# Modulation vectors in a two-layer streaming-encoder trunk: where the sums of the last gates are computed, and how the attention paces them

## The chip, the cores and the metric

The kernel runs on one core of one Trainium2 chip. A core has five engines that run side by side: TensorE (PE, matrix products into PSUM), VectorE (DVE), ScalarE (ACT), GpSimd (POOL) and SyncE (SP), which here issues every DMA. Each engine runs its own instructions strictly in order and waits on semaphores for the others. The metric is the device time of one execution in microseconds, the median of several runs.

## What is computed

The trunk has two layers over x of 1024 tokens by 1024 channels. Each layer is a token mixer (layer 0: softmax attention with forget gates, 16 heads; layer 1: gated linear attention, GLA, 4 heads) and a SwiGLU channel mixer with 2816 hidden channels. Six modulation vectors per layer come from one conditioning vector c:

```python
c_act = jax.nn.silu(c)
for i in range(DEPTH):
    mod = c_act @ ada_w[i] + ada_b[i]
    sh1, sc1, g1, sh2, sc2, g2 = jnp.split(mod, N_MOD, axis=-1)
    h = modulate(rms_norm(x, norm1_g[i]), sh1, sc1)
    y = forgetting_attention(h, ...) if i == 0 else gated_linear_attention(h, ...)
    x = x + g1[:, None, :] * y
    h = modulate(rms_norm(x, norm2_g[i]), sh2, sc2)
    x = x + g2[:, None, :] * swiglu(h, ffn_w_in[i], ffn_w_out[i])
return rms_norm(x, final_g)
```

The vectors are numbered j = 0 to 5 in the order of the split. Vectors 0 and 1 of a layer are needed before its token mixer, 2 (g1) behind the token mixer, 3 and 4 ahead of the channel mixer's products, and 5 (g2) only at the very end of the channel mixer. Each vector is the product of c_act (1024) with a 1024 x 1024 block of ada_w, 4 MB of float32.

## The kernel before

All large products are made of three float32r products, high x high, high x low and low x high parts (`mm3`, L266 to L270), so each operand is split into a high part (a cast on ACT) and a low part (a subtraction on DVE or POOL): `split` at L173, and `load_w` at L202 for the weights.

The program is one straight list of instructions. Python generators interleave the stages: `weave` mixes two of them by their given costs, and a framework gives every instruction its semaphores and settles each engine's order by a planned timeline, in which earlier instructions of the list go first when they are ready. `in_order` and `issue_after` fix some of it by hand.

In order of time the kernel does the following. A prologue normalizes x, makes vectors 0 and 1 of layer 0 by its own code and starts the projections. The attention goes through 8 pairs of heads; while pair p is computed (`attention(p)`), the projections of pair p + 1 are woven in (`qk_proj` twice, `v_half` between). Each projection has two halves of 512 tokens, 24 matmuls each, and every half is emptied from its PSUM bank by `q_evac` or `k_evac`. Then come the output projection and the channel mixer of layer 0 (`ffn(0, ...)`, products of 12 matmuls in its first phase), the GLA mixer head by head, and the output projection and channel mixer of layer 1 (`ffn(1, ...)`).

The modulation vectors that the prologue doesn't make are computed by `ada_steps` (L397). One vector is a sum over 1024 rows of ada_w, weighted by c_act. A step takes 32 x nt rows of ada_w, whose 1024 columns lie as four groups of 256 on four groups of 32 partitions of a raw tile (four DMAs from SP, L405), and adds nt weighted sums of 128 x 256 on DVE (L424, L426) onto an accumulator; with nt = 4 a vector takes 8 steps, with nt = 2 it takes 16. At the end matmuls with a 128 x 4 matrix (L431) add the partitions into a PSUM tile of the ring `pj`, and DVE adds the bias (L434).

Each `yield` of `ada_steps` hands a cost to `Pace` (L443), which adds the time that a call gives it and runs steps while its balance is not negative. There are two paces:

- `ada0`, in the attention: vectors 2, 3, 4 and 5 of layer 0 with nt = 4 and no loading ahead. A step is a load and its four sums in one go, at a cost of 1.0. Its raw tiles are taken from `wr`, the ring of three tiles through which the weights of the attention also pass (L208). `qk_proj` calls it with 3.3 behind both halves of each of the 12 projections of pairs 2 to 7 (L1079).
- `ada1`, elsewhere: layer 1's vectors with nt = 2. `mid0` queues vectors 0 and 1 in channel mixer 0, behind its plain first tiles, with three raw tiles and two loads ahead, at costs ADA_A = 6.0 ahead of a step's sums and ADA_B = 3.0 behind them. Every product (`prod`) adds 0.64 for each of its three- or four-deep operand blocks, 2.56 in the first phase. GLA queues vectors 2, 3, 4 and 5 with two raw tiles and one load ahead, at costs 2.5 and 1.0. Behind each half projection of GLA 5.1 is added.

Channel mixer 1 computes no modulation vector. The weights of a channel mixer are fetched up to five operands ahead (`feed.depth = 5`); their sums of blocks are POOL's (L815) and their splits ACT's and DVE's (L174, L175).

Of the kernel before, what the change touches and what calls it, by code (L numbers as in the profile page):

```python
# [20 lines left out]
HALF = 512  # L21
# [32 lines left out]
def trunk(ctx, tc, x, c, ada_w, ada_b, norm1_g, norm2_g, ffn_w_in, ffn_w_out,  # L54
# [54 lines left out]
    def psl(t, n=1):  # L109
        return slice(t * P, (t + n) * P)  # L110
# [161 lines left out]
    def proj(ps, w, hs, hf):  # L272

        cs = hsl(hf)
        for k in range(8):
            mm3(ps, w.hi[:, k, :], w.lo[:, k, :], hs[k].hi[:, cs], hs[k].lo[:, cs], k == 0, k == 7)
            yield 0.65
# [106 lines left out]
    def make_a(l, i, ks=slice(0, 8)):  # L384
        j = 1 if i == 0 else 4
        g0 = 96 + i * 16 + l * 8
        nc.vector.scalar_tensor_tensor(amul[:, l, i, ks], modc[:, l, j, ks], 1.0,
                                       vec[:, g0:g0 + 8][:, ks], op0=ALU.add, op1=ALU.mult)

    def last_of(e):  # L390
        return next(i for i in reversed(nc.cur_bb.bb.instructions) if i.engine == ENG[e])

    def ada_steps(l, j, acc, raw_of, nt, ahead):


        steps, got = deque(range(32 // nt)), deque()

        def load():
            if not steps:
                return  # L400
            n = steps.popleft()
            raw = raw_of([P, nt * 256], F32, f"ada{l}{j}{n}").rearrange("p (t c) -> p t c", t=nt)
            src = ada_w[l, 32 * nt * n:32 * nt * (n + 1), j * D:(j + 1) * D]
            for q in range(4):
                nc.sync.dma_start(raw[32 * q:32 * q + 32],  # L405
                                  src[:, 256 * q:256 * q + 256].rearrange("(r t) c -> r t c", t=nt))
            got.append(raw)

        for _ in range(ahead):
            load()  # L410
        for n in range(32 // nt):
            load()
            if ahead:
                yield ADA_A
            raw = got.popleft()
            with ExitStack() as es:
                if ahead:
                    es.enter_context(tc.issue_after(last_of("D")))
                elif n == 0:
                    es.enter_context(tc.issue_after(split_after["D"]))  # L420
                for t in range(nt):
                    o = (0 if nt == 4 else 32) + t * (32 // nt) + n
                    if n == t == 0:
                        nc.vector.tensor_scalar(acc, raw[:, t], c42[:, o:o + 1], None, op0=ALU.mult)  # L424
                    else:
                        nc.vector.scalar_tensor_tensor(acc, raw[:, t], c42[:, o:o + 1], acc,  # L426
                                                       op0=ALU.mult, op1=ALU.add)
            yield ADA_B if ahead else 1.0
        mp = pj([P, 2, 4], F32, f"mp{l}{j}")
        for b in range(2):  # L430
            nc.tensor.matmul(mp[:, b], acc[:, psl(b)], four, start=True, stop=True)  # L431
        o = l * 48 + j * 8
        qb = lambda t: t.rearrange("p (q b) -> p b q", b=2)
        nc.vector.tensor_add(qb(modc[:, l, j]), mp, qb(vec[:, o:o + 8]))  # L434
        for i, jj in ((0, 1), (1, 4)):
            if j == jj:
                make_a(l, i)
        yield 1.0
# [22 lines left out]

    ada0, ada1 = Pace(), Pace()

    def ada1_queue(js, acc, raws_):
        r = Cycle(raws_)
        for j in js:
            ada1.q.append(ada_steps(1, j, acc, r, 2, len(raws_) - 1))

    mk = mrows[2]
    nc.vector.memset(mk, 0.0)  # L470
# [14 lines left out]
    def new_h(nm):  # L485
        return [Pair(big.tile([P, S], FR, tag=H_SL[2 * k], name=f"{nm}h{k}"),
                     big.tile([P, S], FR, tag=H_SL[2 * k + 1], name=f"{nm}l{k}")) for k in range(8)]
# [231 lines left out]
    def qk_tiles(p):  # L719


        at = {nm: qk_free.popleft() for nm in ("QA", "QB", "KA")}
        if p:
            before = qk_at.pop(p - 1)
            at.update(zip(("KB", "KLA", "KLB"), (before[nm] for nm in ("QA", "KA", "KLA"))))
            qk_free.extend(before[nm] for nm in ("QB", "KB", "KLB"))
        else:
            at.update({nm: qk_free.popleft() for nm in ("KB", "KLA", "KLB")})
        qk_at[p] = at
        return {nm: big.tile([P, S], FR, tag=sl, name=f"{nm}{p}") for nm, sl in at.items()}  # L730
# [338 lines left out]
    def qk_proj(p, i):  # L1069

        if i == 0:
            qkt[p] = qk_tiles(p)
        wt = feed.next()
        feed.depth = 3
        for hf in range(2):
            ps = pj([P, HALF], F32, f"qk{i}{p}{hf}")
            yield from proj(ps, wt, hT, hf)
            (k_evac if i else q_evac)(ps, qkt[p], hf)
        if p > 1:  # L1079
            ada0(3.3)  # L1080

    oTs = {}

# [108 lines left out]
            yield from g  # L1192

    acc0 = acc_r([P, 2, HALF], F32, "acc0")[:, 0, 0:256]
    for j in (2, 3, 4, 5):
        ada0.q.append(ada_steps(0, j, acc0, wr, 4, 0))
    run(v_half(0, 0, gates_end))
    q_evac(accs[1][1][1], qkt[0], 1)
# [4 lines left out]
    for p in range(7):  # L1203
        parts = [qk_proj(p + 1, 0), qk_proj(p + 1, 1)]
        if p < 6:
            parts.insert(1, v_half(p // 2 + 1, p % 2))
        weave(attention(p), 23.0, chain(*parts), 31.0 if p < 6 else 20.8, LAGS)
        load_cum(2 * p + 2)
        load_cum(2 * p + 3)
# [3 lines left out]
    def dump(name, tiles):  # L1213
        if name in dbg:
            for k in range(8):
                nc.sync.dma_start(dbg[name][k], tiles[k])
# [56 lines left out]
    oh = new_h("oh")  # L1273
    x_slots = idle + [list(otr.q)[-1]]
    xs = [big.tile([P, S], F32, tag=x_slots[k], name=f"x0_{k}") for k in range(8)]
# [24 lines left out]
    def ffn_slots(sl):  # L1300
        assert len(sl) == 19
        ex_sl[:] = sl[16:]
        return {"to": sl[0:4], "b": sl[4:12], "hid": sl[12:16]}
# [410 lines left out]
    slots = ffn_slots(rest)  # L1714
# [4 lines left out]
            hs1.extend(new_h("h1"))  # L1719
        return norm_half(xs, ss, hs1, 1, hf, Ring(psp, ["b3", "b4"]), tmp)  # L1720

    def mid0():
        v = Views(slots["hid"], 2, [HALF], "ad0").v
        ada1_queue((0, 1), v[0][:, 0:256], v[1:4])

    ADA_A, ADA_B = 6.0, 3.0
    ffn(0, oh, xs, slots, "fo", mid0, norm_mixer)
    h1 = hs1
    dump("xb0", xs)
    x_d = tc.dram_tile([8, P, S], F32, name="x_d")  # L1730
# [15 lines left out]
    athl = Ring(big, take(1))  # L1746
    s_slot, on_slot = take(2)
    ada_v = Views(take(2), 2, [HALF], "ad").v
    ada1_queue((2, 3, 4, 5), ada_v[0][:, 0:256], ada_v[1:3])
    ADA_A, ADA_B = 2.5, 1.0  # L1750
    rm = ada_v[3]
    nc.vector.memset(rm, 1.0)
    nc.vector.memset(rm.rearrange("p (n c) -> p n c", c=P)[:, :, 0:1], 0.0)
# [247 lines left out]
    oh = new_h("gh")  # L2001
# [8 lines left out]
    xs = [big.tile([P, S], F32, tag=x_slots[k], name=f"x1_{k}") for k in range(8)]  # L2010
# [4 lines left out]
    slots = ffn_slots(rest)  # L2015
# [31 lines left out]
            fzs.append(Views(H_SL[8:16], 2, [HALF], "fz"))  # L2047
        return fzs[0]()

    ffn(1, oh, xs, slots, "go", lambda: None, final_norm, final_scale)  # L2050
    dump("xb1", xs)

# [28 lines left out]
```

## Time and profile before

| what | us |
|---|---|
| median of 3 runs (2403.37, 2404.3, 2410.52) | 2404.3 |
| the profiled execution | 2412.89 |
| its span, from the first to the last instruction | 2411.2 |
| ACT o_s L174, casts of weights, 376 instructions | 217.1 |
| DVE o_s L175, their low parts, 376 instructions | 318.4 |
| ada_s loads, 128 of 128 KB | 2.9 to landing |
| ad_s loads, 384 of 64 KB | 2.4 to landing |

A group of the profile names a line, an engine, an operation and the tiles out<-in, without buffer numbers: `ada_s` is a raw tile of the attention's steps, `ad_s` one of the others' (and `acc_s`, `ad_s` the accumulators), `p_b` a PSUM bank of a channel mixer's product, `s_b` one of attention scores, `kd` GLA's decayed keys, `o_s` split weights of a channel mixer. Behind the bar stand the busy time and the mean of one; then the idle time of the engine before them and who ended it. In views of waits the columns are the total, the number and the longest, in us. A PE that is busy by the profile is not PE at its peak, since the ends of matmuls are modelled.

The stages in the span: the prologue until about 118 us, the attention until about 600 with the output projection from about 480 on, channel mixer 0 until about 1270, GLA until about 1640, its output projection until about 1740 and channel mixer 1 until the end.

### The profile page before, as it was taken

How to read it: one execution, taken by the hardware profiler on the slowest of the kernel's cores; microseconds unless marked ns; L12 is line 12 of the kernel's file. 1: busy time of each engine (PE TensorE's matmuls, PEld its weight loads, DVE VectorE, ACT ScalarE, POOL GpSimd, SP SyncE). 2: the span in 40 equal slices, each digit the busy share in tenths (PEclk: the TensorE clock that was granted, in tenths of full speed). 3: DMA queues.
4: the chain of work that ended last, by engine and by line, in shares of the span. 5: the costliest groups of instructions: out<-in, count | busy, mean ns of one | idle time of the engine just before them, and what ended most of it. 6: DMA issues, size and time to landing. Idle time of an engine off the chain costs nothing.

```text
span 2411.2 us, 35815 instructions
## 1 busy us (share of the span) xinstructions
PE 2376.2 (99%) x12344; PEld 2020.9 (84%) x12344; DVE 1768.2 (73%) x3018; ACT 1128.9 (47%) x2164; POOL 1007.6 (42%) x909
## 2 busy tenths in 40 slices
PE   8999999999999999999999999999999999999998
PEld 7888888888888888888888888888888888888878
DVE  6577778876698788875797676665586767666787
ACT  6666556674443333344325555443343343345326
POOL 1333333333446666643354221222345656653262
PEclk8999999999999999999999999999999999999999
DMA  8432424341435544557654243334324434347664
GB/s 260 137 97 88 124 87 123 107 150 68 149 110 182 176 159 163 181 207 260 228 168 151 76 134 93 100 118 163 122 86 163 171 127 153 131 178 258 230 200 149
DMA packets 335774, 363.43 MB, mean 151 GB/s; under 512 B 24348, under 2 KB 277432, under 8 KB 335592
## 3 DMA queue, kind: packets, MB, share of 16 engines
q1 hardware_dynamic: 335592, 361.15, 45.6%
q8 instruction: 97, 1.59, 0.3%
q14 instruction: 85, 0.70, 0.1%
HBM read 268.19 MB, written 92.86 MB: 150 GB/s over the span
## 4 chain that ended last, share of the span: by engine, by line
PE 79%; DVE 9%; DMA 4%; issue 2%; ACT 2%; SPq 2%; POOL 1%; DVEq 0%; POOLq 0%; ACTq 0%
PE p_b L268 15%; PE p_b L269 15%; PE p_b L270 15%; PE o_b L1150 2%; PE t_b L1136 2%; PE qk_b L268 2%; PE qk_b L269 2%; PE qk_b L270 2%; DMA ad_s<-in_ada_w_dram 1%; PE vps_b L268 1%; PE vps_b L270 1%; PE vps_b L269 1%; SPq L405 1%; PE s_b L1104 1%; PE s_b L1105 1%
## 5 line engine op out<-in xcount | busy, mean ns | idle before, releaser
L174 ACT CAST o_s<-xv_s 128x512 fp32r<-128x512 f32 (+1 forms) x376 | 217.1, 587 | 314.3 <-PE p_b L270 256.1
L175 DVE TENSOR_TENSOR o_s<-xv_s,o_s 128x512 fp32r<-128x512 f32 (+1 forms) x376 | 318.4, 850 | 60.8 <-ACT o_s L174 60.1
L269 PE MATMUL p_b<-B,o_s 128*128 128x512 f32 x608 | 238.6, 392 | 0.0
L270 PE MATMUL p_b<-B,o_s 128*128 128x512 f32 x608 | 237.9, 392 | 0.0
L268 PE MATMUL p_b<-B,o_s 128*128 128x512 f32 x608 | 237.3, 393 | 0.0
L1116 POOL TENSOR_SCALAR lp_s<-lp_s,st 128x128 f32<-128x128 f32 (+7 forms) x128 | 99.0, 778 | 293.4 <-DVE st L1115 280.4
L815 POOL TENSOR_TENSOR ex_s<-xv_s,xv_s 128x512 f32<-128x512 f32 (+1 forms) x64 | 86.8, 1357 | 279.4 <-DMA xv_s<-in_ffn_w_in_dram 112.2
L269 PE MATMUL p_b<-T,o_s 128*128 128x512 f32 x480 | 186.7, 389 | 0.0
L268 PE MATMUL p_b<-T,o_s 128*128 128x512 f32 x480 | 186.7, 389 | 0.0
L270 PE MATMUL p_b<-T,o_s 128*128 128x512 f32 x480 | 181.1, 389 | 0.0
L270 PEld LDWEIGHTS p_b<-B,o_s 128*128 128x128 f32 x608 | 115.2, 190 | 24.1
L268 PEld LDWEIGHTS p_b<-B,o_s 128*128 128x128 f32 x608 | 115.3, 190 | 23.9
L269 PEld LDWEIGHTS p_b<-B,o_s 128*128 128x128 f32 x608 | 115.3, 190 | 23.8
L1114 ACT ACTIVATE lp_s<-lp_s,st 128x128 f32<-128x128 f32 (+7 forms) x128 | 99.3, 776 | 67.0 <-DVE st L1110 64.1
L174 ACT CAST pt_s<-t_b 128x512 fp32r<-128x512 f32 (+1 forms) x160 | 79.7, 548 | 74.7 <-PE t_b L1136 74.0
L1491 DVE TENSOR_TENSOR ex_s<-ex_s,p_b 128x512 f32<-128x512 f32 x140 | 93.7, 680 | 26.9 <-PE p_b L270 26.9
L817 POOL TENSOR_TENSOR xv_s<-ex_s,xv_s 128x512 f32<-128x512 f32 (+1 forms) x64 | 85.6, 1338 | 64.7 <-DVE o_s L175 62.3
L227 POOL TENSOR_TENSOR w_l_s<-w__s,w_h_s 128x256 fp32r<-128x256 f32 x90 | 70.6, 813 | 93.7 <-ACT w_h_s L223 60.4
L175 DVE TENSOR_TENSOR pt_s<-t_b,pt_s 128x512 fp32r<-128x512 f32 (+1 forms) x160 | 96.2, 631 | 15.8 <-ACT pt_s L174 15.1
L268 PEld LDWEIGHTS p_b<-T,o_s 128*128 128x128 f32 x480 | 90.1, 188 | 18.7
L270 PEld LDWEIGHTS p_b<-T,o_s 128*128 128x128 f32 x480 | 90.1, 188 | 18.7
L269 PEld LDWEIGHTS p_b<-T,o_s 128*128 128x128 f32 x480 | 90.1, 188 | 18.6
(1956 smaller groups left out, 7395.4 us busy)
## 6 DMA issues: line engine op xcount, KB each, us to landing
xv_s<-in_ffn_w_in_dram SPq DMA_DIRECT2D x176, 256.0 KB, 3.2
hid_B<-x SPq DMA_DIRECT2D x70, 512.0 KB, 2.6
ad_s<-in_ada_w_dram SPq DMA_DIRECT2D x384, 64.0 KB, 2.4
hid_T<-x SPq DMA_DIRECT2D x36, 512.0 KB, 2.8
xv_s<-in_ffn_w_out_dram SPq DMA_DIRECT2D x96, 192.0 KB, 5.0
ada_s<-in_ada_w_dram SPq DMA_DIRECT2D x128, 128.0 KB, 2.9
xv_s<-in_ffn_w_out_dram SPq DMA_DIRECT2D x40, 256.0 KB, 2.9
T2o<-hid_T SPq DMA_DIRECT2D x18, 512.0 KB, 8.3
```

Source lines behind the costliest of these rows:

```text
L174: nc.scalar.copy(hi, src)
L175: nc.vector.tensor_sub(lo, src, hi.bitcast(F32))
L227: (nc.gpsimd if i < 3 else nc.vector).tensor_sub(lo[:, cs], rw[:, cs], hi[:, cs].bitcast(F32))
L268: nc.tensor.matmul(ps, ah, bh, start=start, stop=False)
L269: nc.tensor.matmul(ps, ah, bl, start=False, stop=False)
L270: nc.tensor.matmul(ps, al, bh, start=False, stop=stop)
L815: nc.gpsimd.tensor_add(s1, a21, a22)
L817: nc.gpsimd.tensor_sub(a11, s1, a11)
L1114: nc.scalar.activation(lp, lp, AF.Exp, bias=mcur, scale=-1.0, accum_out=st[:, qi, 2:3])
L1116: nc.gpsimd.tensor_scalar(lp, lp, st[:, qi, 3:4], 1.0, op0=ALU.mult, op1=ALU.mult)
L1136: nc.tensor.transpose(tp[:, i, :], lps[qi][:, psl(2 * b + jj)], ident)
L1491: nc.vector.tensor_add(d, d if src is None else dest(G, src), ps)
```

## The change

`ada_steps` without loading ahead now gives its cost of 1.0 between the load and the sums, and 0.0 behind the sums. `qk_proj` calls `ada0` behind each half with 1.2, so one step at a time is due, and the load of a step is issued one call before its sums. Vector 5 of layer 0 leaves the attention for channel mixer 0, where it is the first of three and is made with nt = 2. Vector 5 of layer 1 leaves GLA for channel mixer 1. The costs become 4.0 and 2.0 in channel mixer 0, 3.0 and 1.2 in GLA, 12.0 and 6.0 in channel mixer 1.

```diff
         for n in range(32 // nt):
             load()
-            if ahead:
-                yield ADA_A
+            yield ADA_A if ahead else 1.0
             raw = got.popleft()
...
-            yield ADA_B if ahead else 1.0
+            yield ADA_B if ahead else 0.0
...
-    def ada1_queue(js, acc, raws_):
+    def ada1_queue(ljs, acc, raws_):
         r = Cycle(raws_)
-        for j in js:
-            ada1.q.append(ada_steps(1, j, acc, r, 2, len(raws_) - 1))
+        for l, j in ljs:
+            ada1.q.append(ada_steps(l, j, acc, r, 2, len(raws_) - 1))
...
             (k_evac if i else q_evac)(ps, qkt[p], hf)
-        if p > 1:
-            ada0(3.3)
+            if p > 1:
+                ada0(1.2)
...
-    for j in (2, 3, 4, 5):
+    for j in (2, 3, 4):
         ada0.q.append(ada_steps(0, j, acc0, wr, 4, 0))
...
-    def mid0():
-        v = Views(slots["hid"], 2, [HALF], "ad0").v
-        ada1_queue((0, 1), v[0][:, 0:256], v[1:4])
-
-    ADA_A, ADA_B = 6.0, 3.0
-    ffn(0, oh, xs, slots, "fo", mid0, norm_mixer)
+    def mid(*ljs):
+        v = Views(slots["hid"], 2, [HALF], f"ad{ljs[0][0]}").v
+        ada1_queue(ljs, v[0][:, 0:256], v[1:4])
+
+    ADA_A, ADA_B = 4.0, 2.0
+    ffn(0, oh, xs, slots, "fo", lambda: mid((0, 5), (1, 0), (1, 1)), norm_mixer)
...
-    ada1_queue((2, 3, 4, 5), ada_v[0][:, 0:256], ada_v[1:3])
-    ADA_A, ADA_B = 2.5, 1.0
+    ada1_queue([(1, j) for j in (2, 3, 4)], ada_v[0][:, 0:256], ada_v[1:3])
+    ADA_A, ADA_B = 3.0, 1.2
...
-    ffn(1, oh, xs, slots, "go", lambda: None, final_norm, final_scale)
+    ADA_A, ADA_B = 12.0, 6.0
+    ffn(1, oh, xs, slots, "go", lambda: mid((1, 5)), final_norm, final_scale)
```

## The prediction

> **What bounds the kernel now.** I read the first lines of the page first, and then a table by stage: the attention up to its last projections, channel mixer 0, the GLA mixer, channel mixer 1, and the steady middle of mixer 0.
>
> ```profile
> span 2411.2 us, 35815 instructions
> ...
> PE 2376.2 (99%) x12344; PEld 2020.9 (84%) x12344; DVE 1768.2 (73%) x3018; ACT 1128.9 (47%) x2164; POOL 1007.6 (42%) x909
> ```
>
> ```profile
> 118.00:480.00 362.00, 356.04 (x2344) 314.82 (x2343) 282.06 (x731) 216.20 (x465) 134.21 (x184) 1.00 0.34 105
> ...
> 640.00:1270.00 630.00, 629.65 (x2786) 521.44 (x2785) 500.98 (x682) 244.31 (x436) 321.74 (x226) 0.99 0.54 183
> 1270.00:1640.00 370.00, 360.29 (x2142) 318.89 (x2141) 249.40 (x451) 186.59 (x391) 93.75 (x107) 0.99 0.39 114
> ...
> 1740.00:2360.00 620.00, 619.12 (x2735) 512.23 (x2735) 454.27 (x600) 239.38 (x424) 319.75 (x224) 0.99 0.49 169
> ```
>
> ```profile
> 720.00:1020.00 300.00, 300.00 (x1329) 248.47 (x1328) 246.09 (x324) 112.09 (x196) 187.15 (x127) 1.00 0.52 171
> ```
>
> The columns after the stretch and its length are the busy times of PE, PE's weight loads, DVE, ACT and POOL, then the granted clock. PE is the bound: it idles 35.0 us of the span (2411.2 - 2376.2). The channel mixers leave almost nothing to win (0.35 us of 630, 0.88 us of 620). The attention stretch loses 362 - 356.0 = 6.0 us and GLA 370 - 360.3 = 9.7 us. No change to DVE's work can win much more than these two figures, plus what the clock loses after a stall. I then read who PE waits for in each of the two stages.
>
> ```profile
> PE t_b L1136 <- POOL lp_s L1116: 2.4, 2, 1.6
> PE s_b L1104 <- DVE st L1110: 2.2, 5, 1.2
> PE vps_b L268 <- DVE QB L739: 1.2, 1, 1.2
> PE qk_b L268 <- DVE QB L739: 0.7, 1, 0.7
> ```
>
> ```profile
> PE kdt_b L1869 <- DVE kdl_s L175: 2.7, 2, 2.0
> PE ogt_b L1905 <- DVE on_t L1943: 2.2, 3, 1.4
> PE kv_b L268 <- ACT kdh_s L174: 1.7, 1, 1.7
> ```
>
> The first fence is the attention, the second GLA (us in total, times, longest). These are few, single stalls, most of them behind DVE. What does DVE itself wait for? In the whole kernel, for the modulation weights:
>
> ```profile
> DVE ad_s L426 <- DMA ad_s<-in_ada_w_dram: 36.8, 27, 4.1
> ...
> DVE acc_s L426 <- DMA ada_s<-in_ada_w_dram: 16.9, 12, 2.7
> ```
>
> The upper row lies wholly in GLA (the same view cut to 1320 to 1640 us shows the same 36.8 us in 27 waits), the lower one in the attention. DVE runs its instructions in order, so everything queued behind a waiting modulation sum waits as well.
>
> **The change, part by part.** The prices first, from the view of the two raw tiles (the attention's steps of four sums, then the others' steps of two):
>
> ```profile
> L405 SPq DMA_DIRECT2D ada_s<-in_ada_w_dram x128: 560/597/1901, 136.7 to 467.6; - x128
> L426 DVE SCALAR_TENSOR_TENSOR acc_s<-ada_s,c,acc_s x124: 461/484/1228, 142.0 to 475.1; 128x256 f32<-128x256 f32 x124
> ...
> DMA to landing us min/median/max: 2.6/2.9/4.5
> ```
>
> ```profile
> L405 SPq DMA_DIRECT2D ad_s<-in_ada_w_dram x384: 560/592/1595, 691.9 to 1624.8; - x192
> ...
> DMA to landing us min/median/max: 2.2/2.4/5.8
> ```
>
> *Attention.* One gate vector of four leaves: 8 steps of four sums, 32 x 0.484 = 15.5 us of DVE, and 32 DMAs, 32 x 0.597 = 19.1 us of SP. The other 24 steps go from three or four behind each projection (Pace 3.3 a call) to one behind each half projection, and a step's sums come one call after its load. A half projection is 24 matmuls, at the 300 / 1329 = 0.226 us of the middle of mixer 0 that is 5.4 us, and attention work is woven in; four issues (2.4 us) and the landing (2.9 us) are 5.3 us. So the wait of 16.9 us should be nearly gone. What does PE get of it? Two places show the mechanism.
>
> ```profile
> 285.65 3.60 DVE L426 SCALAR_TENSOR_TENSOR acc_s<-ada_s,c,acc_s 128x256 f32<-128x256 f32 x7
> ```
>
> ```profile
> 292.92 0.33 PE L1104 MATMUL s_b<-KA,QA 128*128 128x128 f32 x1 [1.23 <-DVE st L1110]
> ```
>
> ```profile
> 355.17 0.48 DVE L426 SCALAR_TENSOR_TENSOR acc_s<-ada_s,c,acc_s 128x256 f32<-128x256 f32 x1 [1.38 <-DMA ada_s<-in_ada_w_dram]
> ```
>
> ```profile
> 293.50:296.90 3.40, 3.40 (x15) 3.02 (x15) 2.15 (x8) 1.53 (x5) 1.07 (x2) 0.50 0.42 157
> ...
> 1624.70:1628.10 3.40, 3.40 (x12) 2.72 (x10) 2.72 (x5) 0.52 (x1) 0.00 (x0) 0.50 0.54 155
> ```
>
> Seven sums in a row hold DVE for 3.6 us, the score reduction (L1110) comes late, PE waits 1.23 us, and in the next 3.4 us the granted clock is 0.50, which loses half of them, 1.7 us: 2.9 us together. The second is the wait of 1.38 us for a load at 355.2: the reciprocal behind it is late, POOL scales lp late, and PE waits the 1.6 us of the longest POOL row. With the other four waits for L1110 (2.2 - 1.2 = 1.0 us, I count half) the stage holds 2.9 + 1.6 + 0.5 = 5.0 us. A step now holds DVE for at most 4 x 0.49 = 2.0 us in a row, which is still something: I take 4.0. From below it is nothing, from above the stage's whole loss, 6.0 + 1.7 = 7.7 us. The waits of projections for DVE's QB stay: the closing matmuls of a gate (L431) take one of two PSUM banks, so the next half has to take the bank just being emptied. That happens three times instead of four, and I count nothing for it. What is late next is ACT's exp, on which the reciprocals wait.
>
> The raw tile now lies in the ring of three (wr) for a whole call, and this ring also feeds the weight loads. By the order of calls, one weight load in each pair, the first v weight, gets a buffer whose sums are issued only one half projection later. It is loaded three feeds ahead of its use, some three half projections, over 16 us, so I cost this at nothing.
>
> *GLA.* One gate leaves here too: 16 steps, 32 sums (15.5 us of DVE), 64 DMAs (64 x 0.592 = 37.9 us of SP); the other 48 steps come every 4.2 units instead of 3.5. A call adds 5.1 units, and the calls are 5 + 4 + 3 for head 0, then 4 + 4 + 4 a head. Three gates need 3 x (16 x 4.2 + 1) = 204.6 units, so the last starts in call 40, which ends the v projections of the last head. Before, 228 units reached call 45, in the last head's gate projection. So the last head is free of sums. That is where the largest wait sits:
>
> ```profile
> 1618.40 0.92 DVE L426 SCALAR_TENSOR_TENSOR ad_s<-ad_s,c 128x256 f32<-128x256 f32 x1 [2.14 <-DMA ad_s<-in_ada_w_dram]
> ```
>
> ```profile
> 1624.27 0.76 PE L1869 MATMUL kdt_b<-ident,t_s 128*128 128x128 f32 x4 [1.98 <-DVE kdl_s L175]
> ```
>
> DVE waits 2.1 us for a load, splits kd late, and PE waits 2.0 us and then runs 3.4 us at clock 0.50: 3.7 us, which I take in full. The kv stall has another road, through SP:
>
> ```profile
> 1360.29 11.16 SPq L405 DMA_DIRECT2D ad_s<-in_ada_w_dram  x16
> 1371.55 0.53 SPq L209 DMA_DIRECT2D wv_s<-in_gla_w_in_dram  x1
> ```
>
> ```profile
> 1375.87 1.14 ACT L223 CAST wv_4h_s<-wv_s 128x512 fp32r<-128x512 f32 x2 [5.02 <-DMA wv_s<-in_gla_w_in_dram]
> ```
>
> Sixteen modulation DMAs stand ahead of a weight load, ACT idles 5.0 us for it with the kd split behind, and PE waits 1.7 us. The queue gets thinner, not empty: I count half, 0.8. Of the other kd wait (0.7 us) and of the output transposes' 2.2 us I count 0.5, since two of these follow no sum. GLA: 3.7 + 0.8 + 0.5 = 5.0 us, from nothing to 9.7 + 1.7 = 11.4.
>
> *Channel mixers.* Mixer 0 goes from 32 to 48 steps over the same stretch (3 x (16 x 6 + 1) = 291 units against 2 x (16 x 9 + 1) = 290, a product of four matmul groups giving 2.56), so 32 more sums, 15.5 us of DVE, and 64 DMAs, 37.9 us of SP. What hides them: DVE is busy 246.1 us of 300 in the middle, PE 300.0, and DVE waits for no modulation load there, since that queue runs two loads ahead of its sums. The added sums bring DVE to some 261 of 300. Mixer 1 gets 16 steps where it had none, at a third of that rate. I cost both at nothing; if DVE's cover were gone it would be up to 15.5 us in each. The four closing matmuls of a gate only move.
>
> *Sum.* 4.0 + 5.0 = 9.0, less one new stall in the reordered stages, which I price at 1.7 us (as the kv wait): 7.3 us. Against the profiled execution's 2412.9 us (span 2411.2 and 1.7 around it) that is 2405.6. That execution lies 8.6 us above the median of 2404.3, so the forecast for the median is **2397.0 us**.
>
> **The clock.** The two rows at clock 0.50 follow gaps of 1.2 and 2.0 us. The Trainium skill ("TensorE: Matmul & The Clock Gate", "HAM oscillation — how this bites in real kernels") warns only of idle gaps over some 3.4 us. By that rule the removed stalls would give back no clock, 3.4 us less, 2400.4; the two rows speak against it, and I give it 0.03.
>
> **The rivals.**
>
> *The stalls move (0.20).* DVE is freed, but PE's next wait in each place is behind ACT's exp or POOL. For it: the output transposes wait 1.4 us for DVE with no sum near. Against it: four of the seven stall rows above lead to a sum or its load. Then only the last head's 3.7 us or less stay: 2400.6 to 2404.3.
>
> *Mixer 0's weights come late (0.15, slower).* Its SP queue now issues four modulation DMAs every 2.3 products instead of every 3.5. The place is POOL's sum of two weight blocks, which already waits for loads in the middle of mixer 0:
>
> ```profile
> POOL ex_s L815 <- DMA xv_s<-in_ffn_w_in_dram: 38.1, 12, 5.4
> ```
>
> The price of a late weight is the kv row's, 1.7 us, and 1.7 of clock. It decides from the third on (7.3 / 3.4 = 2.1); late at every third of the 16 added steps, five times, it is 17.0 - 7.3 = 9.7 us more than before, 2414.0. Against it: weights are fetched five products ahead (feed.depth), and PE misses nothing there now. The Trainium skill ("DMA: Bandwidth & Descriptors", "Rules for kernel authors") says to coalesce transfers, as those under 64 KB are mostly overhead. By that rule this gate, going from 32 pieces of 128 KB to 64 of 64 KB, should cost; the trace agrees as far as SP's time (592 ns against 597 for half the bytes), not in landing (2.4 us against 2.9).
>
> *Nearly all of the loss goes (0.10).* If the shorter DVE queue also ends the small waits, the gain is 13 to 19 us (7.7 + 11.4 as the most): 2385 to 2391.
>
> **How the numbers follow.** The forecast has 0.52, with its own range of 4 to 11 us gained, 2393.3 to 2400.3; the rivals have 0.20, 0.15, 0.10 and the clock's rule 0.03. A measurement tells about 0.3%, 7.2 us, from no change, so the bound is 2397.1: 0.30 of the forecast and the 0.10 lie beyond, faster 0.40. Slower is the late weights, 0.15; the same is the rest, 0.45. The range 2389 to 2407 leaves out most of the slow rival and the far end of the fast one, under 0.2.
>
> **What would show it.** Right: the attention's wait of DVE for these loads falls below 4 us and GLA's below 20; no run of seven sums; no window at clock 0.50 near 293 or 1625; PE busy 300.0 in 720 to 1020 us with DVE near 261. Wrong: PE waits for o or xv tiles in mixer 0, or the idle time of PE in the two stages stays at 6.0 and 9.7 us with other releasers' names.

## The result, and the profile after

| kernel | median us (range, runs) |
|---|---|
| before | 2405.91 (2403.05 to 2410.52, 6) |
| changed | 2419.43 (2416.82 to 2421.24, 6) |

The ratio is 1.005 [1.0039, 1.006]: the change costs some 13 us, and the forecast of 2397.0 was wrong in sign. The profiled execution of the changed kernel took 2420.66 us.

These are the first lines of its page.

```profile
span 2418.9 us, 35804 instructions
...
PE 2375.5 (98%) x12344; PEld 2014.7 (83%) x12344; DVE 1804.2 (75%) x3018; ACT 1131.0 (47%) x2164; POOL 1013.9 (42%) x909
```

DVE executes the same 3018 instructions as before, and yet is busy 36 us longer (1804.2 against 1768.2). So instructions have become longer, though none was added. PE idles 43.4 us instead of 35.0. The table by stage, and the middle of mixer 0, show where (columns as before: PE, its weight loads, DVE, ACT, POOL, granted clock).

```profile
118.00:480.00 362.00, 359.37 (x2382) 317.91 (x2380) 279.44 (x716) 222.53 (x480) 134.93 (x186) 1.00 0.32 97
640.00:1270.00 630.00, 620.07 (x2724) 507.55 (x2723) 517.38 (x692) 237.53 (x423) 321.85 (x224) 0.99 0.56 186
1270.00:1640.00 370.00, 359.12 (x2131) 318.14 (x2130) 240.11 (x425) 186.89 (x388) 98.53 (x107) 0.99 0.35 106
1740.00:2360.00 620.00, 618.88 (x2746) 512.20 (x2745) 480.00 (x631) 245.06 (x432) 321.59 (x226) 1.00 0.52 177
```

```profile
720.00:1020.00 300.00, 290.87 (x1262) 235.79 (x1261) 258.70 (x336) 106.61 (x186) 176.00 (x118) 0.99 0.52 170
```

The attention idles 2.6 us instead of 6.0, as the forecast wanted. GLA idles 10.9 instead of 9.7. Mixer 0, which idled 0.35 us, now idles 9.9, nearly all of it between 720 and 1020 us. Mixer 1 is unchanged. How long mixer 0 takes is read from the starts of its first and one of its last products, in the view of the tile `p_b` (the columns are min/median/max in ns, then first and last start). First before, then after.

```profile
L268 PE MATMUL p_b<-B,o_s x304: 387/389/774, 649.5 to 1088.2; 128*128 128x512 f32 x152
...
L268 PE MATMUL p_b<-T4o,o_s x36: 389/389/395, 1093.9 to 1251.5; 128*128 128x512 f32 x36
```

```profile
L268 PE MATMUL p_b<-B,o_s x304: 387/389/632, 644.2 to 1100.0; 128*128 128x512 f32 x152
...
L268 PE MATMUL p_b<-T4o,o_s x36: 389/389/398, 1105.7 to 1261.4; 128*128 128x512 f32 x36
```

The mixer begins 5.3 us earlier than before and ends 9.9 us later: 617.2 us instead of 602.0. Those 15 us are the whole loss and a little more, since the stages ahead give something back. Nearly all of it is waiting: 9.6 us as the profile draws PE's idle time, and some 12.7 us counted from one matmul's start to the next, which otherwise stand 0.23 us apart. The clock has no part in the difference, since both executions have 6.8 us at 0.50 in the mixer. The waits of PE between 640 and 1270 us name the engine; before, this view had a single row of 0.3 us.

```profile
PE p_b L268 <- DVE x L1490: 5.2, 7, 1.9
PE p_b L268 <- DVE sg_s L1490: 2.8, 6, 0.8
PE mp_b L430 <- DVE ad_s L425: 1.0, 1, 1.0
```

PE waits for banks that DVE has not emptied (L1490 is L1491 of before: it adds a product from PSUM onto its tile in SBUF), not for weights.

The views of PE's waits in the attention and in GLA, and DVE's waits for modulation loads:

```profile
PE t_b L1135 <- POOL lp_s L1115: 0.7, 1, 0.7
PE qk_b L268 <- DVE QB L738: 0.7, 1, 0.7
...
PE s_b L1103 <- DVE st L1109: 0.3, 1, 0.3
```

```profile
PE ogt_b L1904 <- DVE on_t L1942: 2.8, 4, 1.2
PE go_b L268 <- ACT S_t L174: 2.0, 1, 2.0
PE kv_b L268 <- ACT kdh_s L174: 1.5, 1, 1.5
```

```profile
DVE ad_s L425 <- DMA ad_s<-in_ada_w_dram: 23.4, 15, 3.0
...
DVE acc_s L425 <- DMA ada_s<-in_ada_w_dram: 18.4, 12, 2.5
```

In the attention the rows of the forecast shrank. In GLA the `kd` row is gone, and rows of the same size stand in its place.

### The profile page after: what moved, and what is told of

Same layout as the page of the kernel before. It is cut to its first block, busy times and chain, and to the rows that moved or that the text cites. A ratio compares the mean times of both kernels' runs of the same rounds, so it can differ in the third digit from the quotient of the medians.

```text
span 2418.9 us, 35804 instructions
## 1 busy us (share of the span) xinstructions
PE 2375.5 (98%) x12344; PEld 2014.7 (83%) x12344; DVE 1804.2 (75%) x3018; ACT 1131.0 (47%) x2164; POOL 1013.9 (42%) x909
## 4 chain that ended last, share of the span: by engine, by line
PE 46%; DVE 7%; issue 3%; DMA 3%; POOL 2%; ACT 1%; SPq 0%; DVEq 0%; POOLq 0%; ACTq 0%
PE p_b L270 10%; PE p_b L269 10%; PE p_b L268 10%; DVE o_s L175 1%; DVE ad_s L425 1%; PE gr_b L268 1%; PE gr_b L269 1%; PE gr_b L270 1%; PE gv_b L268 1%; PE gv_b L269 1%; PE gv_b L270 1%; DMA xv_s<-in_ffn_w_out_dram 1%; DMA ad_s<-in_ada_w_dram 1%; POOL x L1685 1%; DVE x L1683 1%
## 5 line engine op out<-in xcount | busy, mean ns | idle before, releaser
L268 PEld LDWEIGHTS p_b<-T,o_s 128*128 128x128 f32 x480 | 90.1, 188 | 22.4 <-issue 2.6
L1490 DVE TENSOR_TENSOR ex_s<-ex_s,p_b 128x512 f32<-128x512 f32 x140 | 93.8, 680 | 19.3 <-PE p_b L270 19.0
L270 PEld LDWEIGHTS p_b<-T,o_s 128*128 128x128 f32 x480 | 90.2, 188 | 18.8
L826 POOL TENSOR_TENSOR xv_s<-xv_s,xv_s 128x512 f32<-128x512 f32 x40 | 54.1, 1353 | 123.5 <-issue 70.5
```

The lines of the kernel that those rows point to most:

```text
L268: nc.tensor.matmul(ps, ah, bh, start=start, stop=False)
L270: nc.tensor.matmul(ps, al, bh, start=False, stop=stop)
L826: nc.gpsimd.tensor_sub(r[A12], r[A12], r[A11])
L1490: nc.vector.tensor_add(d, d if src is None else dest(G, src), ps)
```

## The experiments

Theory: mixer 0 loses because its modulation sums, now three steps per seven products, meet POOL's work, are stretched there and make DVE late with the banks. The rivals are the mixer's loads (late weights), the bare number of sums, too few banks, and a loss elsewhere through the new order.

### One part at a time

The first four kernels split the change. The first is the changed kernel with vector 5 of layer 0 left in the attention, at 1.6 a call so that four vectors fit.

```diff
-                ada0(1.2)
+                ada0(1.6)
-    for j in (2, 3, 4):
+    for j in (2, 3, 4, 5):
-    ADA_A, ADA_B = 4.0, 2.0
-    ffn(0, ..., lambda: mid((0, 5), (1, 0), (1, 1)), norm_mixer)
+    ADA_A, ADA_B = 6.0, 3.0
+    ffn(0, ..., lambda: mid((1, 0), (1, 1)), norm_mixer)
```

> The changed kernel, but layer 0's vector 5 stays in the attention (one step per half projection, 1.6 a call) and mixer 0 is as before. Theory, the loss is made in mixer 0 by vector 5's sums: PE is busy 300.0 of 300 us from 720 to 1020 again, and the time is 2406 or a few us less, about 13 us below the changed kernel's 2419. Rival, the loss comes from the new order in the attention or in GLA: 2415 or more.

The second is the kernel before with only that vector moved (the attention keeps its bursts).

```diff
-    for j in (2, 3, 4, 5):
+    for j in (2, 3, 4):
-    ADA_A, ADA_B = 6.0, 3.0
+    ADA_A, ADA_B = 4.0, 2.0     # and mid0 queues (0,5), (1,0), (1,1)
```

> The kernel before with one edit: layer 0's vector 5 goes into mixer 0 (costs 4.0 and 2.0); the attention keeps its bursts with three vectors, GLA its four. Theory: PE loses about 9 us from 720 to 1020 waiting for DVE's additions, and the time is 2415 to 2420. Rival: within 3 us of 2406.

The third is the kernel before with only the new pace of the attention: the cost between load and sums, a call behind each half, four vectors.

```diff
-        if p > 1:
-            ada0(3.3)
+            if p > 1:
+                ada0(1.6)
```

> The kernel before with one edit: the attention's four vectors go one step per half projection (1.6 a call), the sums one call behind the load. The forecast counted 4 us of gain for the attention with one vector less; with all four I expect 2 to 4 us less than 2406. Rival, the stalls only move: within 1.5 us of 2406.

The fourth is the kernel before with only layer 1's vector 5 moved from GLA to mixer 1.

```diff
-    ada1_queue((2, 3, 4, 5), ...)
-    ADA_A, ADA_B = 2.5, 1.0
+    ada1_queue([(1, j) for j in (2, 3, 4)], ...)
+    ADA_A, ADA_B = 3.0, 1.2
-    ffn(1, oh, xs, slots, "go", lambda: None, final_norm, final_scale)
+    ADA_A, ADA_B = 12.0, 6.0
+    ffn(1, oh, xs, slots, "go", lambda: mid((1, 5)), final_norm, final_scale)
```

> The kernel before with one edit: layer 1's vector 5 goes from GLA into mixer 1 (12.0 and 6.0), GLA has three vectors at 3.0 and 1.2. The forecast counted 5 us of gain: 2401. Rival, GLA's loss stays at about 10 us under other names, as the changed kernel's 359.1 busy of 370 (360.3 before) hints: within 2 us of 2406. If mixer 1 suffers as mixer 0 does, above 2408.

In the tables of this section the kernel before was run again beside each set of kernels; its median stands in the head.

| part | median us (before beside it 2407.73) | ratio |
|---|---|---|
| all but vector 5 of layer 0 | 2415.46 | 1.0031 [1.002, 1.0043] |
| only vector 5 of layer 0 | 2422.63 | 1.0064 [1.0051, 1.0076] |
| only the attention's pace, 1.6 | 2411.42 | 1.0021 [1.0011, 1.0031] |
| only layer 1 | 2408.36 | 1.0002 [0.9993, 1.0011] |

The moved vector alone costs 14.9 us, as much as the whole change. Its middle of mixer 0 shows the same gap as the changed kernel's:

```profile
720.00:1020.00 300.00, 289.48 (x1253) 234.18 (x1253) 256.12 (x332) 106.18 (x186) 173.45 (x116) 0.99 0.53 171
```

In the other three PE is busy 300.00 there. Layer 1's move is worth nothing, though GLA loses 32 sums by it. Two expectations failed. The first kernel was to come back to 2406 us, and its 2415.46 lies where the rival had it: mixer 0 is whole, but starts at 656.1 us. The third was to gain 2 to 4 us and loses as many. In both the attention's pace of 1.6 with four vectors is a loss, which I return to.

### What in mixer 0 costs the time

What do the sums of mixer 0 look like? These are their groups between 690 and 1040 us (count, busy time, mean ns): before, then after.

```profile
L426 DVE SCALAR_TENSOR_TENSOR ad_s<-ad_s,c,ad_s 128x256 f32<-128x256 f32 x41 | 25.5, 623 | 0.4
L426 DVE SCALAR_TENSOR_TENSOR ad_s<-ad_s,c 128x256 f32<-128x256 f32 x21 | 13.0, 619 | 0.2
L424 DVE TENSOR_SCALAR ad_s<-ad_s,c 128x256 f32<-128x256 f32 x2 | 1.7, 857 | 0.0
```

```profile
L425 DVE SCALAR_TENSOR_TENSOR ad_s<-ad_s,c,ad_s 128x256 f32<-128x256 f32 x62 | 47.8, 771 | 0.7
L425 DVE SCALAR_TENSOR_TENSOR ad_s<-ad_s,c 128x256 f32<-128x256 f32 x31 | 31.2, 1005 | 1.7 <-DMA ad_s<-in_ada_w_dram 1.5
L423 DVE TENSOR_SCALAR ad_s<-ad_s,c 128x256 f32<-128x256 f32 x3 | 2.1, 688 | 0.0
```

The 64 sums of before took 40.2 us, the 96 of after 81.1: 41 us more, where the forecast had 32 x 0.484 = 15.5. The mean rose from 0.63 to 0.84 us. The timelines of DVE and POOL around 786 us in the changed kernel (start, duration, in us) show how one sum becomes three times as long.

```profile
784.25 0.91 DVE L425 SCALAR_TENSOR_TENSOR ad_s<-ad_s,c 128x256 f32<-128x256 f32 x1
785.09 1.78 DVE L175 TENSOR_TENSOR o013s_s<-ex_s,o013s_s 128x512 fp32r<-128x512 f32 x1
786.79 2.94 DVE L425 SCALAR_TENSOR_TENSOR ad_s<-ad_s,c,ad_s 128x256 f32<-128x256 f32 x2
...
790.86 0.68 DVE L175 TENSOR_TENSOR o_s<-xv_s,o_s 128x512 fp32r<-128x512 f32 x1
...
793.96 0.48 DVE L425 SCALAR_TENSOR_TENSOR ad_s<-ad_s,c,ad_s 128x256 f32<-128x256 f32 x1
```

```profile
784.97 1.36 POOL L1450 TENSOR_TENSOR sg_s<-sg_s,sg_s 128x512 f32<-128x512 f32 x1
786.40 1.62 POOL L1455 TENSOR_TENSOR sg_s<-sg_s,sg_s 128x512 f32<-128x512 f32 x1
788.10 1.36 POOL L1459 TENSOR_TENSOR sg_s<-sg_s 128x512 f32<-128x512 f32 x1
```

While POOL runs one operation behind the other (784.97 to 789.46), two sums take 2.94 us, and a split with both inputs in SBUF takes 1.78. Between POOL's operations a split of the same shape takes 0.68 (790.86) and a sum 0.48 (793.96). DVE is late from there, and some 10 us later PE stops:

```profile
797.72 0.50 PE L268 MATMUL p_b<-B,o_s 128*128 128x512 f32 x1 [1.85 <-DVE x L1490]
```

```profile
783.00:799.00 16.00, 13.88 (x60) 10.92 (x59) 14.72 (x19) 5.83 (x11) 7.61 (x6) 0.99 0.57 189
798.80:802.20 3.40, 3.40 (x10) 2.66 (x9) 0.74 (x2) 0.36 (x1) 1.32 (x2) 0.50 1.12 264
```

In these 16 us DVE is busy 0.92 of the time, against 0.86 over the 300 us; behind the stall the clock is at 0.50 for 3.4 us. Counted over the trace from 690 to 1040 us, the 40 of these two-input sums that start while a POOL operation runs take 1.34 us on average, and the 53 others 0.48, none more than 0.49. Before, 14 of 62 started beside POOL. The Trainium skill ("SBUF — State Buffer", "Who interferes with whom") has the rule: VectorE and GpSimd share a pair of ports as an exclusive lock, and an operation of VectorE with two inputs in SBUF has to wait out a GpSimd operation that reads SBUF and started first, while one with a single SBUF input, outside the two-port modes, doesn't. The durations agree (0.48 us without POOL, up to 1.52 us with it), and the rule suggests a test: put one input of the sum in PSUM.

Four kernels, all made from the changed one. In the first, the running sum of a vector made in mixer 0 or 1 lies in a PSUM bank of `pj`, and only the last sum writes SBUF.

```diff
+                        part = pj([P, 256], F32, f"ap{l}{j}") if ahead == 2 else acc
-                        nc.vector.tensor_scalar(acc, raw[:, t], ...)
+                        nc.vector.tensor_scalar(part, raw[:, t], ...)
+                        last = n == 32 // nt - 1 and t == nt - 1
-                        nc.vector.scalar_tensor_tensor(acc, raw[:, t], c42[:, o:o + 1], acc,
+                        nc.vector.scalar_tensor_tensor(acc if last else part, raw[:, t], c42[:, o:o + 1], part,
```

> The changed kernel, but in the two mixers the running sum lies in a PSUM bank (the last sum writes the SBUF tile), so a sum has one SBUF input. Theory, the sums are stretched (0.48 us alone, up to 1.5 us beside a POOL operation) because both of their inputs are in SBUF: all sums in mixer 0 take about 0.5 us, PE waits for DVE's additions under 3 us in 720 to 1020, and the time falls by 8 to 13 us to 2406 to 2411. Rival, the number of sums or their place in DVE's queue matters: sums get shorter or not, the time stays at 2416 or more.

The second gives the products seven PSUM banks instead of five, for more time before a bank must be empty.

```diff
-        pin, pj = Ring(psp, bk[:5]), Ring(psp, bk[5:])
+        pin, pj = Ring(psp, bk[:7]), Ring(psp, bk[7:])
```

> The changed kernel, but the products of a mixer's first phase rotate over seven PSUM banks instead of five. Theory, DVE is late by 1 to 2 us for stretches of some 15 us and PE feels it through the ring of banks: two more banks are 5.4 us of cover, so most of the waits of p_b for the additions go and the time is 2407 to 2412. Rival, DVE is short of time over the whole stage: 2416 or more.

The third takes away the moved vector's loads after the first three.

```diff
-            for q in range(4):
+            for q in range(4 if (l, j) != (0, 5) or n < 3 else 0):
```

> The changed kernel, but in mixer 0 vector 5's loads are left out after the first three (the sums run on old rows, so that vector is wrong). Theory, DVE's time is the cost: 2417 to 2420, no change. Rival, the forecast's, SP's queue and late weights: 2406 to 2410.

The fourth keeps the loads and takes away the moved vector's sums after the first step.

```diff
-                for t in range(nt):
+                for t in range(nt if (l, j) != (0, 5) or n == 0 else 0):
```

> The changed kernel, but in mixer 0 vector 5's sums are left out after the first step (its loads stay, that vector is wrong). Theory: PE is busy 300 of 300 us from 720 to 1020, time 2404 to 2408. Rival, loads and SP's queue: 2416 or more.

| changed kernel with | median us (before beside it 2406.18) | ratio |
|---|---|---|
| sums in PSUM | 2403.18 | 0.9985 [0.9976, 0.9994] |
| seven banks | 2416.9 | 1.0044 [1.0031, 1.0056] |
| no loads of the moved vector | 2418.87 | 1.0054 [1.0041, 1.0067] |
| no sums of the moved vector | 2414.53 | 1.0031 [1.002, 1.0042] |

The middle of mixer 0 for the first, third and fourth, and the sums of the first:

```profile
720.00:1020.00 300.00, 300.00 (x1330) 248.60 (x1329) 247.51 (x353) 113.27 (x194) 190.98 (x128) 1.00 0.56 183
```

```profile
L427 DVE SCALAR_TENSOR_TENSOR ap_b<-ad_s,c,ap_b 128x256 f32<-128x256 f32 x90 | 43.2, 480 | 0.8
```

```profile
720.00:1020.00 300.00, 289.10 (x1261) 234.54 (x1260) 259.00 (x336) 105.93 (x185) 176.04 (x118) 1.00 0.49 160
```

```profile
720.00:1020.00 300.00, 292.79 (x1281) 238.49 (x1280) 240.55 (x312) 109.16 (x188) 178.82 (x121) 1.00 0.54 174
```

With one input in PSUM the 96 sums take 46 us instead of 81, none is stretched although 55 of them start beside a POOL operation, and PE misses nothing. DVE's other instructions stand in the changed kernel's order there, and all but a few sums at the same places among them, so it is the stretching that this edit took away. The kernel is then 3 us faster than before, the best of all that ran; 16 us came back where 8 to 13 were expected. Leaving out the moved vector's loads saves nothing: late weights were not the cause.

More banks give back little or nothing. Whether DVE lacks time rather than depth is not shown by that, since the edit also leaves `pj` one bank instead of three and changes the planned order of DVE's work; its sums take 0.92 us on average.

The fourth result goes against my simple form of the theory: without the moved vector's sums 66 are left, hardly more than before, and most of the loss stays. The number of sums is not it either. But where the sums are left out the loss is gone: from 720 to 820 us, most of vector 5's time, PE misses 0.3 us instead of 2.9, and from 820 to 1020 us 6.9 instead of 6.2.

### The place of the sums

What did remain in that kernel is the pace. Seven products are one group of hidden channels, 7 x 2.56 = 17.92 units. Costs of 4 + 2 put three steps at nearly the same places of every group, 6 + 3 put two. So the third set has a kernel before with only mixer 0's costs changed (64 sums, both vectors of before):

```diff
-    ADA_A, ADA_B = 6.0, 3.0
+    ADA_A, ADA_B = 4.0, 2.0
```

> The kernel before with one edit: mixer 0's two vectors at costs 4.0 and 2.0 instead of 6.0 and 3.0; 64 sums as before, three steps in a group of seven products instead of two. Theory, it matters where the sums fall beside POOL's work: their mean goes from 0.63 us towards the 0.84 us of the changed kernel, mixer 0 gets about 8 to 12 us longer, time 2413 to 2418. Rival, the number of sums matters: within 3 us of 2406.

the changed kernel with the sums 2 units (some 2 us) earlier at the same rate:

```diff
-    ADA_A, ADA_B = 4.0, 2.0
+    ADA_A, ADA_B = 2.0, 4.0
```

> The changed kernel with mixer 0's costs 2.0 and 4.0 instead of 4.0 and 2.0: as many sums at the same rate, 2 units (0.8 of a product) earlier in the group. Theory, the place beside POOL's work matters: the mean of the sums moves from 0.84 us by more than 0.1, and mixer 0's time goes the same way, by 5 us or more. Rival, the rate alone matters: mean 0.8 to 0.9 us and 2417 to 2421 again.

the changed kernel with the attention's pace at 1.6, three vectors:

```diff
-                ada0(1.2)
+                ada0(1.6)
```

> The changed kernel with 1.6 instead of 1.2 a call in the attention: three vectors as there, but two steps in some calls. With four vectors 1.6 made the attention 3.5 to 5.6 us longer than before. If that is the pace, the attention is 431 to 435 us long by its trace and the time 4 to 8 us above the changed kernel's; if it is the fourth vector, 427 us and no change, 2419.

and the kernel before once more, for a second trace of it:

> The kernel before, unedited, for a second trace. If the stalls that the forecast priced are the kernel's own, PE waits again 2.0 us for kd in the last head of GLA and 1.2 us for the score reduction near 292 us, each with a window at clock 0.50 behind it, and GLA takes 352 to 353 us; if they belong to that one execution, GLA takes 348 to 350 us, as in two kernels with the same GLA code.

| kernel | median us (before beside it 2406.91) | ratio |
|---|---|---|
| before, mixer 0 at 4 + 2 | 2418.76 | 1.0052 [1.0039, 1.0065] |
| changed, mixer 0 at 2 + 4 | 2406.6 | 1.0002 [0.9993, 1.0011] |
| changed, attention at 1.6 | 2427.03 | 1.0086 [1.0072, 1.01] |
| before again | 2405.88 | 0.9998 [0.9989, 1.0007] |

The middle of mixer 0 of the first two, with the last two thirds of it and the sums for the first, and the sums of the second:

```profile
720.00:1020.00 300.00, 292.88 (x1278) 239.38 (x1277) 243.70 (x315) 110.09 (x192) 176.24 (x119) 0.99 0.51 164
```

```profile
820.00:930.00 110.00, 106.06 (x465) 86.12 (x464) 93.55 (x124) 39.31 (x69) 66.15 (x44) 1.00 0.52 171
930.00:1020.00 90.00, 90.00 (x399) 74.53 (x398) 63.71 (x80) 35.04 (x60) 56.22 (x38) 1.00 0.41 142
```

```profile
L426 DVE SCALAR_TENSOR_TENSOR ad_s<-ad_s,c,ad_s 128x256 f32<-128x256 f32 x41 | 29.5, 719 | 0.5
L426 DVE SCALAR_TENSOR_TENSOR ad_s<-ad_s,c 128x256 f32<-128x256 f32 x21 | 22.5, 1071 | 0.1
```

```profile
720.00:1020.00 300.00, 296.62 (x1309) 244.15 (x1308) 273.29 (x346) 110.32 (x193) 187.99 (x127) 1.00 0.57 182
```

```profile
L425 DVE SCALAR_TENSOR_TENSOR ad_s<-ad_s,c,ad_s 128x256 f32<-128x256 f32 x62 | 38.0, 613 | 0.4
L425 DVE SCALAR_TENSOR_TENSOR ad_s<-ad_s,c 128x256 f32<-128x256 f32 x31 | 30.4, 982 | 0.1
```

These stretches are the lesson of the case. Without a single added sum, the pace alone costs 12 us, and the 64 sums take 53.7 us with their openings instead of 40.2. DVE's mean, 243.70 of 300 where before had 246.09, hides it: at this pace the sums end at 925 us, up to 930 us DVE is busier than before (180.0 of 210 us against 170.3), and all that PE misses lies there. With all 96 sums 2 us earlier, DVE is busy 273.29, more than in any other kernel here but one, and PE loses 3.4 us instead of 9.1; the kernel is level with before. So the busy share decides little.

What does decide is shown in part. At 2 + 4, 29 sums start beside POOL instead of 40, but DVE's splits of weights are longer (`o_s`, 974 ns on average against 901). New costs also change the planned order of DVE's and ACT's other instructions: in the traces, the kernel before at 4 + 2 has nearly the changed kernel's order in mixer 0, and the changed kernel at 2 + 4 is nearer to that of before. PE shows it too: its first product with `B11o` starts some 16 us ahead of the last with `B` in the changed kernel, in before at 4 + 2 and with sums in PSUM, and 8.4 us ahead in before and at 2 + 4. No run parts the place of the sums from this order. With short sums the order costs nothing, since the kernel with sums in PSUM has the changed kernel's order and PE misses nothing.

The third kernel was to tell the pace of 1.6 from the fourth vector. With three vectors it costs 7.6 us more than 1.2 does (2427.03 against 2419.43), so it is the pace. PE's waits for the reductions in the attention, first of the kernel before with only this pace, then of this one; the changed kernel has 0.3 us:

```profile
PE s_b L1103 <- DVE st L1109: 4.5, 6, 1.5
```

```profile
PE s_b L1103 <- DVE st L1109: 3.0, 4, 1.5
```

At 1.6 some calls have two steps, the sums of the second right behind its own load. That this is what costs the time is argued from the code; no run separates it, and it stays open.

The second trace of before settles a question of the clock. Its span is 2399.5 us, 11.7 less than that of the execution I forecast from. The stalls are there again, the clock's loss isn't:

```profile
292.99 0.33 PE L1104 MATMUL s_b<-KA,QA 128*128 128x128 f32 x1 [1.06 <-DVE st L1110]
```

```profile
293.00:296.40 3.40, 3.40 (x23) 3.06 (x24) 3.20 (x12) 2.54 (x8) 0.74 (x2) 1.00 0.45 166
1617.00:1620.40 3.40, 3.04 (x16) 2.61 (x17) 2.54 (x6) 0.03 (x1) 0.00 (x0) 1.00 0.32 96
```

A stall of 1.06 us is followed by clock 1.00 here, where 1.23 us at the same place was followed by 0.50; the 1.64 us of `kd` ahead of the second row likewise. So of what was expected the stalls belong to the kernel, and the windows at 0.50 to the execution. Mixer 0 takes 598.6 us here, with no such window in it.

## Why the prediction was wrong

*The step that failed* is the channel mixers': "I cost both at nothing; if DVE's cover were gone it would be up to 15.5 us in each." In mixer 1 that held (PE 618.88 of 620, 32 sums added). In mixer 0 it cost some 15 us; with the 5.0 us that GLA did not give, these are 20 of the 22 us between forecast and result. That 15 is also the upper end named there is chance: DVE's sums in mixer 0 grew by 41 us, and how much of it reached PE hung on the pace. The cover was read from an average, 246 of 300, and the price of a sum, 0.484 us, from the attention's steps. The average forecast even came out (261 foreseen, 258.7 measured), by luck, since the sums were longer and fewer of DVE's other operations fell into the same 300 us; it said nothing. The rows that could have warned were there: even the attention's sums reach 1228 ns beside a median of 484, and those of mixer 0 already averaged 0.63 us before. The new pace laid more of them beside POOL (40 of 93 instead of 14 of 62), among the additions that empty the banks.

*The rival on the slow side* had the sign, the stage and nearly the time (2414.0), but not the mechanism. PE waits for banks, not for weights, and without the loads the time is the same.

*The attention* was right in direction. PE idles 3.3 us less between 118 and 480 us, and mixer 0's first product starts at 644.2 us instead of 649.5 (647.8 in the second trace of before), so its share is some 3.3 to 5.3 us, against 4.0 forecast. The longest run of sums is four instead of seven, as foreseen. But DVE's wait for the loads, which should have fallen below 4 us, went from 16.9 to 18.4. The timelines of SP and DVE in the changed kernel show why:

```profile
138.23 7.61 SPq L405 DMA_DIRECT2D ada_s<-in_ada_w_dram  x8
```

```profile
143.15 0.35 DVE L423 TENSOR_SCALAR acc_s<-ada_s,c 128x256 f32<-128x256 f32 x1 [1.20 <-DMA ada_s<-in_ada_w_dram]
...
149.85 1.53 DVE L425 SCALAR_TENSOR_TENSOR acc_s<-ada_s,c,acc_s 128x256 f32<-128x256 f32 x3 [2.49 <-DMA ada_s<-in_ada_w_dram]
```

The loads of two steps leave in one train, and DVE is ready for the first sum 3.7 us behind the first issue (143.15 - 1.20 - 138.23), where I had counted 5.4 for the call and 5.3 for issues and landing. In nine of the 24 steps DVE is ready within some 4 us of the first issue. Loads a call ahead in the list are less than that ahead in time. What became less are PE's waits for the reductions (`st`, 2.0 us to 0.3 between 90 and 525 us), which fits the shorter runs of sums. The smaller number of sums is not the reason: the kernel with only vector 5 moved has as few, in the old bursts, and still waits 1.5 us there and idles 5.8 us between 118 and 480 us.

*GLA* was forecast at 5.0 us and gave nothing. The `kd` stall is gone and DVE's waits fell to 23.4 us, not quite below the 20 foreseen, but PE idles as long as before, now behind ACT (`S_t`, 2.0 us). That is the rival "the stalls move", in this stage; moving layer 1's vector alone gave 1.0002.

*The clock.* No window at 0.50 stands near 293 or 1625 us, as forecast: the granted clock of the changed kernel is 1.00 from 293 to 297 and from 1624.7 to 1628.1 us. It proves nothing, since the second trace of before has none there either. The 3.4 us of clock in the sum were the price of one execution, 8.6 us above its median; gains and losses of that kind are to be counted at part of their size.

## What to carry to other kernels

Before moving work to an engine "with room", look at pieces as short as the buffers between it and the bound engine (here five banks of 2.7 us a product, so some 15 us, not 300), and price an operation from rows of the place where it will run, not from where it runs now. Where VectorE and GpSimd both work on SBUF, try accumulators in PSUM: here it took 35 us off 96 sums and turned a loss of 0.5% into a gain of 0.15%. An interleaving by costs has a phase as well as a rate, and here also moves the planned order of everything else; try the phase before giving a move up.

## What the runs showed of the hardware

A weighted sum of 128 x 256 with both inputs in SBUF takes 0.48 us, and up to 1.52 us beside a tensor operation of POOL; with one input in PSUM it takes 0.48 us either way (mean of 90: 480 ns). Additions that read PSUM (L1490) stay at 0.68 us in the timelines. The operation that opens a vector (L423, a product with one input in SBUF) takes 0.34 us, and once 1.38 us beside POOL; no run here tests why.

A stall of PE of 1 to 2 us is followed by 3.4 us at clock 0.50 in some executions and not in others, at the same place of the same kernel. In the trace of before that the forecast used, nothing at 0.50 follows the stalls of 1.64 us at 358 us and of 1.69 us at 1377 us, and 6.8 us at 0.50 begin at 658.7 us, though PE is busy without a gap from 640 us on. The Trainium skill ("TensorE: Matmul & The Clock Gate", "HAM oscillation — how this bites in real kernels") warns of idle gaps over some 3.4 us; here a window at 0.50 followed one of 1.23 us once. Its section "What's actually happening" calls the window of some 3.4 us free-running, so that its place differs from run to run; the variation seen here agrees with that.
